# A two-layer decoder step on one core: page table loaded early, GpSimd's layer-1 weight parts in quarters, transfers issued by SyncE

## The chip, the core and the metric

The kernel runs on one core of one Trainium2 chip. The core has five engines, each with an instruction stream of its own, which the document calls as the profile does: PE (TensorE, matrix products), DVE (VectorE), ACT (ScalarE), POOL (GpSimd) and SP (SyncE, which only starts transfers here). Transfers between the chip's memory and the core's own (DMA) are started by an instruction on SP, ACT or POOL and then run by themselves; an engine whose next instruction is the start of a transfer that may not start yet stands still until it may. The metric is the device time of one execution in microseconds (us), and less is better. The numbers are medians of several executions; the profile is of one more execution.

## What is computed

One step of a decoder with two layers, for a prompt of 512 tokens and for 8 sample sequences of 4 new tokens with a past of 1024, all in float32, model width 1024:

```
for layer in range(2):
    h = rms_norm(x, norm_mix[layer])
    z = h @ w_in                                   # one projection for everything in the layer
    t = hgrn2(z) if layer == 0 else sparse_attention(z)   # 6 heads of 128
    c = memory_attention(z)                        # 4 heads of 64 over 256 memory rows
    x = x + concat(t, c) @ w_out[layer]
    h = rms_norm(x, norm_ffn[layer])
    u = h @ w_gate                                 # width 2816
    y = (silu(causal_conv3(u)) * (h @ w_up)) @ w_down
    x = x + y

# sparse_attention, for the samples
ik_past = cache_idx_k[page_table]                  # 8 pages of 128 rows a sequence
score   = sum_h iw[h] * relu(iq[h] . ik)           # then the 256 best rows of a token are chosen
k, v    = cache_k[page_table], cache_v[page_table] # and attention goes over the chosen rows
```

Layer 0's mixer is a gated linear recurrence over chunks of 32 tokens. In layer 1 each token's indexer scores choose the 128 (prompt) or 256 (samples) rows that its attention sees; the keys, values and indexer keys of the past lie in pages, and a table of 64 entries says where. The memory rows of the prompt are projected in each layer, and those of the samples come from a cache. Beside x, the step returns the new keys, values, states and convolution rows.

## The kernel before, in words

The residual x lies feature-major in eight tiles of 128 features by 544 tokens (32 sample tokens, then 512 of the prompt). All weights are one list of 199 units of 128x1024 float32, in the order of their use. `Weights` (716) loads a unit at most three ahead into `raw`, ACT copies it into `whi` in a format of less precision, and the rest, `wlo = raw - whi`, is made by DVE or POOL; `part` (753) says by which. A product over such a unit is three passes on PE (`mm3`): `a<-hi,whi`, `a<-lo,whi` and `a<-hi,wlo`, and these are the bulk of the trace.

The program is written out instruction by instruction, and nothing reorders it afterwards: an engine executes its own in the order in which the Python code reaches them. Two kinds of code call the engines. The main stream goes through the projections. Generators, each a head or a part of one, lie in `Pump` (495) and are moved on between the main stream's products. Which one comes next, and whether DVE or POOL makes a `wlo`, is decided at build time by `Model` (225), a set of clocks moved on by rough costs. `Pump.run`, `finish`, `space` and `drain` are the places at which the main stream lets generators go on.

Weights are loaded by SP, in layer 1 by POOL (`W.queue, W.lead = G, LEAD1`, 1625; back at 2145). Other transfers of the places at hand:

- `sample_kv` (1161) loads keys and values of the cached memory, two transfers for each of eight sequences and each layer, issued by ACT (`S`); `mem_load` (960) the prompt's memory; `ffn` (1180) the convolution's state `cst`. Layer 1's new keys, values and indexer keys (`k_p`, `v_p`, `ik_p` and their `_s`) and two small tables (`tt`, `ex`) also go by ACT.
- The page table is loaded between layer 0's `out_proj` (1172) and the norm before its FFN (1575 to 1593): once as it is into all partitions (`ptb`, 64 entries), and by eight transfers into `ptv`, 16 partitions each. DVE makes row numbers from both, `iidx` for the gathers of indexer keys and `vidx` for those of values. The norm's last part, `Norm._finish` (934), comes behind: column sums on PE, 1/sqrt on DVE (`m__finish`, `rs`), its spread over the partitions on PE (`rb__finish`).
- In layer 1, `sample_scores` (1905) loads 64 key pages by SP (`key_page`, 1600), each by an address that SP reads out of `ptb`, two groups ahead, while attention of the prompt, the selection of rows (`choose_sample`, 1755) and the memory attention run as generators.

In the rows every helper records its instructions at line 398, so the names of the tiles say which step it is.

Of the kernel before, what the change touches and what calls it, by code (L numbers as in the profile page):

```python
# [7 lines left out]
F32 = mybir.dt.float32  # L8
# [25 lines left out]
# ---------------------------------------------------------------- host layout  # L34
# [43 lines left out]
def weight_units(i, order):  # L78
    """the weight blocks in the order in which the program asks for them"""
# [128 lines left out]
TURNS = 2          # selections at work at a time  # L208
# [13 lines left out]
NUNITS = 199  # L222


class Model:
# [89 lines left out]
    def room(self, g, gens):  # L315
        """from when a generator's next step finds the tiles that it takes"""
# [25 lines left out]
    def held_up(self, n, eng):  # L342
        """until when other engines are at work on the part of a tile that is to be written"""
# [58 lines left out]
def place(busy, t, took):  # L402
    """the first time from t on when something is free for so long"""
# [11 lines left out]
def extent(ap):  # L415
    """first and last column and partition of an operand in its tile"""
# [78 lines left out]
class Pump:  # L495
    """Generators of instructions beside the main stream. A generator yields, before each step, the tiles that
    the step reads (None: all that it has given out so far); a step is given out once they are ready."""
    def __init__(self, model):
        self.turn = 0
        self.m, self.gens, self.dv, self.names, self.urgent = model, [], [], {}, []  # L500
# [1712 lines left out]
```

## Time and profile before

| what | value |
|---|---|
| time, median of 3 runs | 1492.95 us (1491.08 to 1493.73) |
| span of the profiled execution | 1500.7 us |
| PE busy | 1434.9 us, 96% |
| DVE, ACT, POOL busy | 803.2, 587.5, 567.3 us |
| layer 0 up to its out_proj | 0 to about 347 us |
| layer 0's FFN | about 353 to 750 us |
| layer 1 up to its out_proj | 750 to about 1050 us |
| layer 1's out_proj and FFN | 1050 to 1500 us |

The profile is of one execution, whose span is 0.5% above the median of the timed runs. Busy times of engines overlap, so they don't add up to the span; what counts is where PE is idle and whom it waits for there. A row of a timeline is a run of like instructions on one engine: when it started, how long it took, the engine, the operation, what it writes `<-` what it reads, how many, and in brackets how long the engine was idle before and what ended that.

### The profile page before, as it was taken

The page shows a single profiled execution, that of the slowest core. Times are in us where ns is not written, and L with a number is a line of the kernel's source. Part 1 is how long each engine was busy: PE and PEld are TensorE (multiplying, and loading weights), DVE is VectorE, ACT ScalarE, POOL GpSimd, SP SyncE. Part 2 cuts the span into 40 slices and gives each one's busy share as a digit, 9 for nine tenths or more (in the row PEclk, how much of TensorE's full clock was granted, in tenths as well). Part 3 has the DMA queues.
Part 4 walks back from the last instruction along what each step waited for, and adds up shares of the span by engine and source line. Part 5 has one row for each costly group of instructions (what it writes and reads, how often), then busy time and mean ns, then how long its engine had stood idle before and what let it go on. Part 6 is the DMA issues. An engine that isn't in the chain of part 4 may idle for free.

```text
span 1500.7 us, 28191 instructions
## 1 busy us (share of the span) xinstructions
PE 1434.9 (96%) x11314; PEld 1345.6 (90%) x11314; DVE 803.2 (54%) x1762; ACT 587.5 (39%) x1064; POOL 567.3 (38%) x600
## 2 busy tenths in 40 slices
PE   8989999998999999999999797689999999999998
PEld 7978889998999999999987775456999999999998
DVE  7466886653444234444469988867444442244431
ACT  5447466332333123333335443466333331133320
POOL 4422444323444124446753444341134440144410
PEclk9999999999999999999999997989999999999999
DMA  5542132321333223224414236631222323232241
GB/s 186 177 156 64 59 117 86 101 85 62 88 95 93 92 73 94 90 85 126 135 54 131 83 115 202 199 127 57 71 76 89 96 85 99 73 95 87 85 121 57
DMA packets 60145, 152.52 MB, mean 102 GB/s; under 512 B 9040, under 2 KB 22960, under 8 KB 60016
## 3 DMA queue, kind: packets, MB, share of 16 engines
q1 hardware_dynamic: 39456, 110.11, 23.9%
q0 software_dynamic: 8208, 26.50, 5.4%
q10 hardware_dynamic: 12352, 14.13, 2.9%
q8 instruction: 89, 1.46, 0.4%
q14 instruction: 40, 0.33, 0.1%
HBM read 142.23 MB, written 8.47 MB: 100 GB/s over the span
## 4 chain that ended last, share of the span: by engine, by line
PE 84%; DVE 11%; issue 2%; ACT 1%; DMA 1%; another core or an unknown queue 0%; ACTq 0%; POOL 0%; SPq 0%; DVEq 0%; POOLq 0%
PE a L398 71%; DVE ple_choose_sample L398 2%; PE u_hgrn_head L398 1%; DVE isc_index_prompt L398 1%; PE id_index_prompt L398 1%; PE mkv L398 1%; PE ao_prompt_attn L398 1%; PE ho_hgrn_head L398 1%; PE ms_prompt L398 1%; PE hgrn_head_samples L398 1%; PE as_prompt_attn L398 1%; DVE t L398 1%; DMA ptv<-pt 1%; DVE lo L398 1%; PE mo_prompt L398 1%
## 5 line engine op out<-in xcount | busy, mean ns | idle before, releaser
L398 PE MATMUL a<-hi,whi 128*128 128x272 f32 x2640 | 556.4, 292 | 1.4 <-DVE t L398 1.0
L398 PE MATMUL a<-lo,whi 128*128 128x272 f32 x2640 | 551.0, 290 | 4.9 <-DVE lo L398 4.6
L398 POOL TENSOR_TENSOR wlo<-raw,whi 128x1024 fp32r<-128x1024 f32 x143 | 342.7, 2397 | 557.3 <-ACT whi L398 551.1
L398 PE MATMUL a<-hi,wlo 128*128 128x272 f32 x2640 | 549.1, 289 | 0.0
L398 PEld LDWEIGHTS a<-hi,whi 128*128 128x128 f32 x2640 | 417.7, 190 | 9.2 <-issue 5.4
L398 PEld LDWEIGHTS a<-lo,whi 128*128 128x128 f32 x2640 | 418.1, 190 | 6.2 <-DVE lo L398 5.6
L398 PEld LDWEIGHTS a<-hi,wlo 128*128 128x128 f32 x2640 | 418.1, 190 | 0.0
L398 ACT ACTIVATE whi<-raw 128x1024 fp32r<-128x1024 f32 (+1 forms) x202 | 209.5, 1038 | 230.9 <-PE a L398 151.3
L398 DVE TENSOR_TENSOR wlo<-raw,whi 128x1024 fp32r<-128x1024 f32 (+1 forms) x59 | 79.7, 1351 | 160.6 <-ACT whi L398 157.7
L398 DVE TENSOR_TENSOR sc<-a,rb 128x544 f32<-128x544 f32 x53 | 38.4, 724 | 116.1 <-PE a L398 114.5
L398 DVE SCALAR_TENSOR_TENSOR conv<-ext,params,conv 128x560 f32<-128x560 f32 x88 | 70.6, 802 | 45.1 <-ACT conv L398 43.6
L398 DVE TENSOR_TENSOR ext<-a,rb 128x240 f32<-128x240 f32 x132 | 37.5, 339 | 105.9 <-PE a L398 102.2
L398 ACT ACTIVATE conv<-ext,params 128x560 f32<-128x560 f32 x44 | 37.6, 855 | 136.2 <-DVE ext L398 132.6
L398 ACT ACTIVATE hi<-sc 128x544 fp32r<-128x544 f32 x44 | 29.0, 658 | 137.3 <-DVE sc L398 137.3
L398 DVE TENSOR_TENSOR x<-a,x 128x544 f32<-128x544 f32 x48 | 34.7, 723 | 80.1 <-PE a L398 72.5
L398 POOL TENSOR_TENSOR sqa<-sqa,sq 128x544 f32<-128x544 f32 x24 | 34.8, 1448 | 110.0 <-ACT sq L398 108.3
L398 DVE TENSOR_TENSOR sc<-sc,conv 128x512 f32<-128x512 f32 x88 | 62.5, 748 | 4.9 <-DVE sc L398 0.5
L398 ACT ACTIVATE conv<-conv 128x560 f32<-128x560 f32 x44 | 29.6, 672 | 73.8 <-DVE conv L398 73.8
L398 ACT ACTIVATE hi<-x,params 128x544 fp32r<-128x544 f32 x32 | 23.9, 745 | 70.4 <-DVE x L398 68.5
L398 DVE TENSOR_TENSOR lo<-sc,hi 128x544 fp32r<-128x544 f32 x44 | 31.9, 725 | 31.9 <-ACT hi L398 31.9
L398 PE MATMUL a<-whi,hi 128*128 128x256 f32 x160 | 46.8, 293 | 0.0
L398 PE MATMUL a<-whi,lo 128*128 128x256 f32 x160 | 45.1, 282 | 0.0
(406 smaller groups left out, 1931.9 us busy)
## 6 DMA issues: line engine op xcount, KB each, us to landing
raw<-w SPq DMA_DIRECT2D x177, 512.0 KB, 3.6
raw<-w POOLq DMA_DIRECT2D x21, 512.0 KB
k_sample_scores<-ckT SPq DMA_DIRECT2D x46, 128.0 KB, 3.5
ck_mem_samples<-cmkT ACTq DMA_DIRECT2D x16, 256.0 KB, 6.2
cv_mem_samples<-cmv ACTq DMA_DIRECT2D x16, 256.0 KB, 4.7
st_s<-hgrn_head_samples POOLq DMA_DIRECT2D x12, 256.0 KB
hgrn_head_samples<-hst SPq DMA_DIRECT2D x10, 256.0 KB, 3.5
ck_sample_scores<-ckT SPq DMA_DIRECT2D x18, 128.0 KB, 2.1
```

The costliest lines, as they stand in the source:

```text
L398: return f(*args, **kw)
```

## The change

Five edits, of which the fourth only removes text (comments).

1. In layer 1, a `wlo` that POOL makes is four instructions of 128x256 instead of one of 128x1024 (`W.piece`). There are 21 of them. Those of DVE, and POOL's in the rest of the program, stay whole.
2. The order of generators is a string (`SCRIPT`), read by `Pump.play`, and `Pump.pick` reads from it which engine takes a `wlo` and two other small steps. Read out engine by engine, PE's order is row for row that of before, and DVE's but for the rows below.
3. The page table comes from the host as one 128x72 array, in which the 64 entries stand in each partition and `ptv`'s eight behind them. One transfer on SP, before layer 0's fifth head, loads it; `page_rows` makes `iidx` and `vidx` ahead of layer 0's `out_proj`.
4. Comments go.
5. All of ACT's transfers but the parameters and rope tables at the start are issued by SP (`Q`), at the same places of the program.

```diff
+    def begin(self, script):
+        self.made = [*self.gens, *self.dv]
+        self.script = iter([c for n, c in re.findall(r"(\d*)(\D)", script) for _ in range(int(n or 1))])
+
+    def play(self):
+        for c in self.script:
+            if c == ".":
+                return
+            g = self.made[LETTERS.index(c)]
+            self.step(g, self.gens if g in self.gens else self.dv)
+
+    def pick(self, c):
+        return c if self.script is None else next(self.script) == "+"
...
     def run(self, *need):
+        if self.script is not None:
+            return self.play()
...
-                (V if model.t["dve"] <= late else G).tensor_sub(lo[:, c:c + n], raw[:, c:c + n], hi[:, c:c + n].bitcast(F32))
+                if pump.pick(model.t["dve"] <= late):
+                    V.tensor_sub(lo[:, c:c + n], raw[:, c:c + n], hi[:, c:c + n].bitcast(F32))
+                    return
+                step = min(n, self.piece)
+                for i in range(c, c + n, step):
+                    G.tensor_sub(lo[:, i:i + step], raw[:, i:i + step], hi[:, i:i + step].bitcast(F32))
...
     def sample_kv(l, b):
         k, v = slot(name="ck"), slot(name="cv")
-        S.dma_start(k[:, :512], a["cmkT"][l, b])
-        S.dma_start(v3(v[:, :512], 2, 256), a["cmv"][l, b].rearrange("(m p) c -> p m c", p=128))
+        Q.dma_start(k[:, :512], a["cmkT"][l, b])
+        Q.dma_start(v3(v[:, :512], 2, 256), a["cmv"][l, b].rearrange("(m p) c -> p m c", p=128))
...
+    def page_rows():
+        p4 = v3(ptb[:, 0:64], 32, 2)
+        for e in range(2):
+            pr = slice(64 * e, 64 * e + 64)
+            V.tensor_scalar(iidx[pr], p4[pr, :, e], 64.0, cc("iota64")[pr], op0=ALU.mult, op1=ALU.add)
+        V.tensor_scalar(vidx[:, 0, :], ptb[:, 64:72], 64.0, cc("iota16"), op0=ALU.mult, op1=ALU.add)
+        for i in range(1, 4):
+            V.tensor_scalar(vidx[:, i, :], vidx[:, 0, :], float(i), None, op0=ALU.add)
...
+        if hd == 4:
+            Q.dma_start(ptb, a["pt"])
...
+    page_rows()
     norm = Norm(gffn[:, 0, :])
     out_proj(0, cat, [*([g] for g in gates), [mg[0], mg[1], mg[4]], mg[2:5]], norm)
     n1 = Norm(gmix[:, 1, :])
-    S.dma_start(ptb, bass.AP(tensor=pt_ap.tensor, offset=pt_ap.offset, ap=[[0, 128], [1, 64]]))
...
-    for s in range(8):
-        S.dma_start(ptv[16 * s:16 * s + 16, :], bass.AP(tensor=pt_ap.tensor, offset=pt_ap.offset + s, ap=[[0, 16], [8, 8]]))
...
-    W.queue, W.lead = G, LEAD1
+    W.queue, W.lead, W.piece = G, LEAD1, 256
...
-            S.dma_start(a["k_p"][256 * i:256 * i + 256].rearrange("(j p) c -> p j c", p=128), v3(kr[i][:, :512], 2, 256))
-        S.dma_start(a["k_s"], kr[2][0:NS, :256])
+            Q.dma_start(a["k_p"][256 * i:256 * i + 256].rearrange("(j p) c -> p j c", p=128), v3(kr[i][:, :512], 2, 256))
+        Q.dma_start(a["k_s"], kr[2][0:NS, :256])
...
-        pt=cont(i["page_table"].reshape(1, 64)),
+        pt=cont(np.concatenate([np.tile(i["page_table"].reshape(1, 64), (128, 1)),
+                                np.repeat(i["page_table"].reshape(8, 8).T, 16, axis=0)], 1)),
```

DVE's order before, at the end of layer 0's out_proj (`x` is the residual, `sqa` the sum of its squares, `m__finish` the norm's rows):

```order
L398 TENSOR_TENSOR x_89<-a_3986,x_89 128x544
L398 SCALAR_TENSOR_TENSOR lo_4037<-x_89,params_79,hi_4036 128x544
L398 TENSOR_TENSOR sqa_3520<-sqa_3520,sq_4038 128x544
L398 TENSOR_SCALAR iidx<-ptb,consts_81 64x32 x2
L398 TENSOR_SCALAR vidx<-ptv,consts_81 128x8
L398 TENSOR_SCALAR vidx<-vidx 128x8 x3
L398 TENSOR_SCALAR m__finish_1_4120<-st__finish_1_4111 128x5
```

And now, at the end of layer 0's heads, where the six rows stand between the gates (`lo_gate`, `sc`) and ahead of the first `x` of out_proj; behind `sqa`, `m__finish` follows at once:

```order
L420 TENSOR_TENSOR sc_3429<-sc_3429,on_hgrn_head_1_3052 128x544
L420 TENSOR_SCALAR iidx<-ptb,consts_81 64x32 x2
L420 TENSOR_SCALAR vidx<-ptb,consts_81 128x8
L420 TENSOR_SCALAR vidx<-vidx 128x8 x3
L420 TENSOR_TENSOR lo_gate_1_3556<-sc_3429,hi_gate_1_3555 128x544
L420 TENSOR_TENSOR sc_3521<-sc_3521,on_hgrn_head_1_3539 128x544
L420 TENSOR_TENSOR lo_gate_1_3592<-sc_3521,hi_gate_1_3591 128x544
L420 TENSOR_TENSOR x_82<-a_3531,x_82 128x544
```

So the six rows moved from ahead of the norm to ahead of out_proj. POOL's order now, in layer 1's projections, where it loads weights (`raw`), makes low parts and the second half of a rotation (`rq`):

```order
L420 TENSOR_TENSOR wlo_9021<-raw_9018,whi_9020 128x256 x4
L420 DMA raw_9114<-w 128x1024
L420 DMA raw_9116<-w 128x1024
L420 DMA raw_9118<-w 128x1024
L420 TENSOR_TENSOR wlo_9133<-raw_9114,whi_9132 128x256 x4
L420 DMA raw_9139<-w 128x1024
L420 TENSOR_TENSOR rq_9268<-rq_9268,t_5_9269 128x544
L420 TENSOR_TENSOR wlo_9275<-raw_9116,whi_9274 128x256 x4
```

Each low part was one row of 128x1024 at the same place. ACT's order before, in layer 1 where the keys are done (`kr`), with the transfers between its own instructions:

```order
L398 ACTIVATE sr_9815<-ss_sample_scores_4_10650 128x256
L398 DMA k_p<-kr_10030 128x2x256
L398 DMA k_p<-kr_10031 128x2x256
L398 DMA k_s<-kr_10032 32x256
L398 ACTIVATE kT_10033<-kT_keys_1_10684 128x512
L398 ACTIVATE kT_10066<-kT_keys_2_10690 128x512
L398 ACTIVATE ktn<-kTn_keys_1_10696 128x64
L398 DMA ck_mem_samples_1_10755<-cmkT 128x512
L398 DMA cv_mem_samples_1_10756<-cmv 128x2x256
```

They moved to SP, whose order there is now (`ck_sample_scores` is a tile of two key pages, and TENSOR_LOAD reads a page's address from the table):

```order
L420 DMA ck_sample_scores_21_10708<-ckT 128x256
L420 DMA k_p<-kr_10066 128x2x256
L420 DMA k_p<-kr_10067 128x2x256
L420 DMA k_s<-kr_10068 32x256
L1659 TENSOR_LOAD ptb
L1659 ISA x2
L420 ISA
L420 DMA ck_sample_scores_22_10748<-ckT 128x256
```

What moved here is that the pages behind now come after the three stores; the first batch of eight `ck` and `cv` of the memory follows four pages later, the second twelve pages after that, and six pages come last.

## Rows read from the trace of the kernel before

**Rows 1.** the page's first part: busy us (share) xinstructions of each engine

```profile
PE 1434.9 (96%) x11314; PEld 1345.6 (90%) x11314; DVE 803.2 (54%) x1762; ACT 587.5 (39%) x1064; POOL 567.3 (38%) x600
```

**Rows 2.** windows: stretch, us, busy of PE PEld DVE ACT POOL, clock, DMA

```profile
340.00:360.00 20.00, 14.95 (x107) 14.24 (x107) 6.36 (x25) 4.89 (x8) 5.29 (x6) 0.83 0.19 63
...
750.00:870.00 120.00, 106.97 (x770) 93.89 (x770) 101.96 (x239) 55.97 (x137) 55.38 (x67) 0.96 0.27 84
870.00:1050.00 180.00, 149.22 (x1073) 104.49 (x1073) 140.23 (x464) 94.88 (x261) 68.75 (x76) 0.89 0.45 146
```

**Rows 3.** chain of waits, 340 to 360 us: start us, us, what

```profile
339.67 9.91 DMA ptv<-pt
```

**Rows 4.** timeline of PE, 345 to 372 us: start us, us, instructions [idle before <- releaser]

```profile
347.10 0.41 PE L398 MATMUL a<-hi,wlo 128*128 128x272 f32 x2
352.57 1.36 PE L398 MATMUL rb__finish<-consts,rs 128*128 128x128 f32 x5 [5.05 <-DVE rs L398]
...
357.58 0.41 PE L398 MATMUL a<-hi,wlo 128*128 128x272 f32 x2
```

**Rows 5.** the same around the second FFN, 1100 to 1112 us

```profile
1105.72 0.41 PE L398 MATMUL a<-hi,wlo 128*128 128x272 f32 x2
...
1108.77 0.41 PE L398 MATMUL a<-hi,wlo 128*128 128x272 f32 x2
```

**Rows 6.** timeline of DVE, 330 to 358 us

```profile
349.65 0.23 DVE L398 TENSOR_SCALAR vidx<-ptv,consts 128x8 int32<-128x8 int32 x1 [10.00 <-DMA ptv<-pt]
```

**Rows 7.** groups of POOL's instructions, 750 to 1050 us: count, busy us, mean ns, idle before

```profile
L398 POOL TENSOR_TENSOR wlo<-raw,whi 128x1024 fp32r<-128x1024 f32 x21 | 50.0, 2383 | 37.6 <-ACT whi L398 37.6
...
L398 POOL TENSOR_TENSOR kr<-v,tt 128x128 f32<-128x128 f32 x8 | 4.5, 601 | 2.8 <-DVE v L398 2.8
```

**Rows 8.** timeline of DVE, 835 to 842 us

```profile
837.70 2.26 DVE L398 TENSOR_TENSOR ple_choose_sample<-consts,ple_choose_sample 128x7 int32<-128x7 int32 x1
```

**Rows 9.** timeline of POOL, 835 to 842 us

```profile
837.54 2.39 POOL L398 TENSOR_TENSOR wlo<-raw,whi 128x1024 fp32r<-128x1024 f32 x1
```

**Rows 10.** timeline of DVE, 888 to 892 us

```profile
890.57 0.16 DVE L398 TENSOR_TENSOR ple_choose_sample<-consts,ple_choose_sample 128x3 int32<-128x3 int32 x1
```

**Rows 11.** timeline of DVE, 757 to 764 us

```profile
759.59 3.43 DVE L398 TENSOR_SCALAR m_index_keys<-m_index_keys 128x5 f32<-128x5 f32 x4
```

**Rows 12.** timeline of DVE, 950 to 968 us

```profile
962.86 3.18 DVE L398 TENSOR_SCALAR p_prompt_attn<-p_prompt_attn,m_prompt_attn 128x256 f32<-128x256 f32 x1
```

**Rows 13.** timeline of DVE, 905.5 to 911 us

```profile
908.88 0.45 DVE L398 TENSOR_TENSOR ple_choose_sample<-ple_choose_sample 128x1 int32<-128x1 int32 x1
```

**Rows 14.** timeline of DVE, 765 to 774 us

```profile
767.94 4.67 DVE L398 TENSOR_TENSOR t_index_keys<-ikt_index_keys,tt 128x32 f32<-128x32 f32 x10
```

**Rows 15.** timeline of POOL, 765 to 774 us

```profile
769.32 2.44 POOL L398 TENSOR_TENSOR wlo<-raw,whi 128x1024 fp32r<-128x1024 f32 x1
```

**Rows 16.** timeline of ACT, 918 to 958 us

```profile
930.26 0.63 ACT L398 ACTIVATE hi<-mem 128x512 fp32r<-128x512 f32 x1 [5.36 <-DMA cv_mem_samples<-cmv]
...
951.94 0.60 ACT L398 ACTIVATE p_prompt_attn<-p_prompt_attn,m_prompt_attn,rqs 128x256 f32<-128x256 f32 x1 [4.82 <-DMA cv_mem_samples<-cmv]
```

**Rows 17.** timeline of PE, 945 to 970 us

```profile
953.59 0.49 PE L398 MATMUL ao_prompt_attn<-pt_prompt_attn,v 128*128 128x128 f32 x2 [2.08 <-ACT pt_prompt_attn L398]
...
964.11 1.25 PE L398 MATMUL ss_sample_scores<-k_sample_scores,qS 128*32 128x256 f32 x15 [0.93 <-ACT ct_prompt_attn L398]
```

**Rows 18.** timeline of SP's transfer issues, 926 to 966 us

```profile
926.87 29.86 SPq L398 DMA_DIRECT2D k_sample_scores<-ckT  x19
```

**Rows 19.** the page's sixth part: issues, KB each, median us from issue to landing

```profile
k_sample_scores<-ckT SPq DMA_DIRECT2D x46, 128.0 KB, 3.5
```

**Rows 20.** timeline of ACT, 36 to 75 us

```profile
68.81 1.06 ACT L398 ACTIVATE whi<-raw 128x1024 fp32r<-128x1024 f32 x1 [4.22 <-DMA cv_mem_samples<-cmv]
```

**Rows 21.** windows in layer 0, columns as in rows 2

```profile
60.00:80.00 20.00, 20.00 (x193) 17.56 (x193) 11.64 (x29) 6.56 (x18) 5.97 (x9) 1.00 0.78 273
```

**Rows 22.** windows around the end of layer 0's heads, columns as in rows 2

```profile
288.00:294.00 6.00, 6.00 (x50) 6.00 (x49) 3.46 (x3) 3.22 (x6) 2.86 (x3) 1.00 0.28 87
```

More of the change, by code (lines that the diff above doesn't have):

```diff
@@ L1 @@
+import re
 import numpy as np
@@ L499, in __init__ @@
         self.turn = 0
+        self.script, self.made = None, []
         self.m, self.gens, self.dv, self.names, self.urgent = model, [], [], {}, []
@@ L504, in make @@
         self.names[name] = n = self.names.get(name, 0) + 1
-        return Gen(it, after, f"{name}{n}", pri, margin)
+        g = Gen(it, after, f"{name}{n}", pri, margin)
+        self.made.append(g)
+        return g
+    def begin(self, script):
[9 more added lines that the diff above has]
+        return c if self.script is None else next(self.script) == "+"
     def add(self, it, after=None, pri=5, margin=0):
@@ L600, in finish @@
     def finish(self, g):
+        if self.script is not None:
+            return self.play()
         while not g.done:
@@ L610, in space @@
     def space(self, tag):
+        if self.script is not None:
+            return self.play()
         m = self.m
@@ L620, in drain @@
     def drain(self):
+        if self.script is not None:
+            return self.play()
         while self.gens:
@@ L640, in program @@
     pump = Pump(model)
+    if plan is not None:
+        pump.begin(SCRIPT)
     uid = {}
@@ L719, in __init__ @@
             self.raw, self.parts, self.kept = {}, {}, {}
-            self.queue, self.lead = Q, LEAD0
+            self.queue, self.lead, self.piece = Q, LEAD0, 1024
             self.whole = list(plan.whole) if plan else []
@@ L861, in scale_rows @@
     def scale_rows(p, r):
-        if model.t["act"] < model.t["dve"]:
+        if pump.pick(model.t["act"] < model.t["dve"]):
             S.activation(p, p, AF.Copy, scale=r)
@@ L951, in scaled @@
         t = slot(name="sc")
-        if model.t["dve"] > max(model.t["pe"], model.t["act"]) + BUSY:
+        if pump.pick(model.t["dve"] > max(model.t["pe"], model.t["act"]) + BUSY):
             S.activation(halves(t), ac, AF.Copy)
@@ L961, in mem_load @@
         t = slot(name="mem")
-        S.dma_start(v3(t[:, :512], 2, 256), a["memT"][:, 2 * len(raw):2 * len(raw) + 2, :])
+        Q.dma_start(v3(t[:, :512], 2, 256), a["memT"][:, 2 * len(raw):2 * len(raw) + 2, :])
         raw.append(t)
@@ L1182, in ffn @@
         cst = slot(name="cst")
-        S.dma_start(cst[:, :NF * 16], a["cst"][l])
+        Q.dma_start(cst[:, :NF * 16], a["cst"][l])
         SE = 514
@@ L1542, in gate @@
         cat[hd] = yield from split_in(sg)
+    ptb = cp.tile([128, 72], I32, name="ptb")
+    iidx = cp.tile([128, 32], I32, name="iidx")
+    vidx = cp.tile([128, 4, 8], I32, name="vidx")
+    def page_rows():
[6 more added lines that the diff above has]
+            V.tensor_scalar(vidx[:, i, :], vidx[:, 0, :], float(i), None, op0=ALU.add)
     memraw = []
@@ L1577, in program @@
     n1 = Norm(gmix[:, 1, :])
-    ptb = cp.tile([128, 64], I32, name="ptb")
-    pt_ap = a["pt"]
-    S.dma_start(ptb, bass.AP(tensor=pt_ap.tensor, offset=pt_ap.offset, ap=[[0, 128], [1, 64]]))
-    iidx = cp.tile([128, 32], I32, name="iidx")
-    p4 = v3(ptb, 32, 2)
-    for e in range(2):
-        pr = slice(64 * e, 64 * e + 64)
-        V.tensor_scalar(iidx[pr], p4[pr, :, e], 64.0, cc("iota64")[pr], op0=ALU.mult, op1=ALU.add)
-    ptv = cp.tile([128, 8], I32, name="ptv")
-    for s in range(8):
-        S.dma_start(ptv[16 * s:16 * s + 16, :], bass.AP(tensor=pt_ap.tensor, offset=pt_ap.offset + s, ap=[[0, 16], [8, 8]]))
-    vidx = cp.tile([128, 4, 8], I32, name="vidx")
-    V.tensor_scalar(vidx[:, 0, :], ptv, 64.0, cc("iota16"), op0=ALU.mult, op1=ALU.add)
-    for i in range(1, 4):
-        V.tensor_scalar(vidx[:, i, :], vidx[:, 0, :], float(i), None, op0=ALU.add)
     def gather(out, src, idx):
@@ L1621, in program @@
     for i, t in enumerate(tt):
-        S.dma_start(t, a["ttab"][:, i, :])
+        Q.dma_start(t, a["ttab"][:, i, :])
     qtab = [tt[j // 4][:, 128 * (j % 4):128 * (j % 4) + 128] for j in range(5)]
     itab = [tt[1][:, 128 + 64 * j:192 + 64 * j] for j in range(5)]
-    W.queue, W.lead = G, LEAD1
+    W.queue, W.lead, W.piece = G, LEAD1, 256
     cat = [None] * 8
@@ L1651, in index_keys @@
         yield from key_rope([ikv], pc("g_ik"), itab, rs, 1, 64, [ikr])
-        S.dma_start(a["ik_p"].rearrange("(j p) c -> p j c", p=128), v3(ikr[:, :256], 4, 64))
-        S.dma_start(a["ik_s"], ikr[0:NS, 256:320])
+        Q.dma_start(a["ik_p"].rearrange("(j p) c -> p j c", p=128), v3(ikr[:, :256], 4, 64))
+        Q.dma_start(a["ik_s"], ikr[0:NS, 256:320])
         b, b2 = bank("ikT"), bank("ikT")
@@ L2114, in program @@
                 ex = slot(name="ex")
-                S.dma_start(ex[0:NS, :256], a["expand"])
+                Q.dma_start(ex[0:NS, :256], a["expand"])
                 V.tensor_copy(eb, ex[0:NS, :256])
@@ L2132, in values @@
                 for i in range(2):
-                    S.dma_start(a["v_p"][256 * i:256 * i + 256].rearrange("(j p) c -> p j c", p=128), v3(row[i][:, :512], 2, 256))
-                S.dma_start(a["v_s"], row[2][0:NS, :256])
+                    Q.dma_start(a["v_p"][256 * i:256 * i + 256].rearrange("(j p) c -> p j c", p=128), v3(row[i][:, :512], 2, 256))
+                Q.dma_start(a["v_s"], row[2][0:NS, :256])
             token_major(proj_tm("dtm", 1024, xs=h), values, 0)
@@ L2144, in program @@
             mem_load(memraw)
-    W.queue, W.lead = Q, LEAD0
+    W.queue, W.lead, W.piece = Q, LEAD0, 1024
     model.keep, model.main = 0, MAIN0
```

21 lines of the change are left out of this document (added).

## The prediction

> **What bounds the kernel now.** The page's first part comes first: TensorE (PE) is busy 1434.9 us of a span of 1500.7 [rows 1], so at most 66 us are to be had unless PE itself runs quicker. The stages say where they lie [rows 2]: PE is busy 14.95 of 20 us at 340 to 360, 106.97 of 120 at 750 to 870 and 149.22 of 180 at 870 to 1050. These lack 5.05, 13.03 and 30.78 us, and their granted clock is 0.83, 0.96 and 0.89, between the two levels of 1.2 and 2.4 GHz: part of PE's busy time there is spent at the lower one. In the two late stretches VectorE (DVE) is nearly as full as PE, 101.96 of 120 and 140.23 of 180, so what DVE waits for counts there.
>
> The first place is a single stall. The chain of waits has the transfer ptv<-pt for 9.91 us from 339.67 [rows 3]; behind it DVE's first vidx instruction has waited 10.00 us and starts at 349.65 [rows 6]; and PE, in the first norm before an FFN, ends its last pair of products of out_proj and waits 5.05 us for DVE's rs [rows 4]. The rest is spread, and I read it by timelines of single engines.
>
> **Page table (term A, -7.4).** The six page instructions stand in DVE's order ahead of the norm's m__finish, so one small late transfer holds the norm. The same norm before the second FFN has none. From the start of the last pair of the output projection to that of the ninth pair behind rb__finish it is 357.58 - 347.10 = 10.48 us in the first [rows 4] and 1108.77 - 1105.72 = 3.05 in the second [rows 5]: the same PE rows, one time with the wait and the low clock that follows it. The difference is 7.43 us. With the wait gone, next late is what the second norm shows, and that leaves no gap. I take -7.4, with 1 us either way.
>
> The table now comes by one transfer on SyncE (SP) at head 4, before the fifth of six heads, and is read behind the sixth. Its six DVE instructions stand between the gates of layer 0; where the heads end PE is busy 6.00 of 6 and DVE 3.46 [rows 22], so I cost them at 0. If a gate behind them were late, they would cost what they take: six times at most the 0.23 of the first vidx [rows 6], some 1.4.
>
> **Quarters (term B, -7).** A DVE instruction that begins as a long GpSimd (POOL) instruction begins ends only with it: 128x7 int32 at 837.70 took 2.26 us [rows 8] while POOL's wlo ran from 837.54 for 2.39 [rows 9], and the same instruction with 128x3 took 0.16 [rows 10]. Of layer 1's 21 wlo on POOL [rows 7] I count 16 that hold a DVE instruction so, by 1.9 to 2.8 us, some 34 us in all; the first held one is in the four of 759.59 that took 3.43 together [rows 11], the last the one of 3.18 at 962.86 [rows 12]. What does a short POOL instruction do? While eight kr of 128x128 run, 601 ns each [rows 7], a DVE instruction of one column took 0.45 [rows 13], so it was held by at most 0.45, not 2.1.
>
> A quarter's time, from two rows of the same operation [rows 7]: (2383 - 601)/(1024 - 128) = 1.99 ns a column, so 601 + 128 x 1.99 = 856 ns, four 3.42 us, 1.04 more than the whole, 22 us on POOL in all. POOL is busy 55.38 of 120 and 68.75 of 180 [rows 2], so this is hidden as long as a weight's low part is not what PE waits for.
>
> What DVE saves depends on what follows the held one. Where it is followed by instructions that POOL does not hold (8 of 16, selection and softmax work as in rows 8), one hold of 2.1 becomes one of about 0.6: 1.5 saved. In two mixed places I take 0.8. In the other six DVE runs through instructions with two inputs, as the ten t_index_keys that took 4.67 [rows 14] across the wlo of 2.44 at 769.32 [rows 15]; there each quarter can hold the next one, and I take 0. DVE saves 8 x 1.5 + 2 x 0.8 = 13.6. Only part is on PE's path: in these 300 us PE lacks 43.8 while DVE lacks 57.8 [rows 2], so neither rules all the time. I take half, -7. The ends are -13.6, and +3, if six dense places lose 0.5 each to more changes of hand.
>
> The Trainium skill (SBUF — State Buffer, Terms) says that the port pair of VectorE and GpSimd is locked exclusively, for a full instruction, and that the loser blocks completely. Rows 8 and 9 agree, 2.26 us against 2.39. By the rule alone four quarters are four locks, and the term would be 0 wherever DVE's work wants those ports throughout.
>
> **ScalarE freed (term C, -2).** ScalarE (ACT) issued eight memory-key and memory-value transfers in a row at two places of layer 1 and stood behind them 5.36 us before 930.26 and 4.82 before 951.94 [rows 16]. Only behind the second does PE wait, 2.08 us before 953.59, for ACT's pt_prompt_attn [rows 17]. That is -2.1; the ends are 0 (something else is late there) and 5.36 + 4.82 = -10.2. In layer 0 ACT stood 4.22 behind such a batch at 68.81 [rows 20], but PE is busy 20.00 of 20 there [rows 21]: 0.
>
> The Trainium skill (DMA: Bandwidth & Descriptors, Issuing engines are not separate DMA queues) says that starting transfers on several engines saves only the time of starting them, usually small beside the transfer. By that the whole term would be near 0; rows 16 show 4.82 us of an engine that was not small.
>
> **SP loaded (term D, +2).** SP now issues these, and they are queued among the key pages of the sample scores. Behind k_p come 19 pages in 29.86 us [rows 18]; two batches of eight and three stores join them. An issue takes at most the even share of ACT's second wait, 4.82/8 = 0.6 us, so 19 x 0.6 = 11.4 us more [rows 16]. The last page is issued by 926.87 + 29.86 = 956.73 and lands 3.5 us later [rows 18, 19]; the group of scores that needs it begins at 964.11 [rows 17], so 964.11 - 956.73 - 3.5 = 3.9 us are spare. If pages are issued without a pause, the queue ends 11.4 later and PE waits 11.4 - 3.9 = 7.5; if SP's present pauses take them up, 0. A page takes 29.86/19 = 1.57 us on average, with its address read into a register, against 0.6 for a plain issue, so pauses for free page tiles are in it, how long the rows don't say. The ends are 0 and +7.5; nearer to the first, since the spare time and the pauses add up, I take +2.
>
> In layer 0 SP's weight loads now stand behind the same batches. The cover is PE's full 20.00 of 20 [rows 21]; if it were gone, it would cost up to the 4.22 us of the batch [rows 20].
>
> **Sum.** -7.4 - 7 - 2 + 2 = -14.4. The profiled execution's 1500.7 us become 1486.3. The median of before, 1492.95, is 0.5% below that execution; the same microseconds from it give **1478.5**.
>
> **Rivals.** *Quarters give nothing.* Each quarter holds a DVE instruction again, as rows 14 and 15 would have it for work with two inputs. For it speaks that POOL's total rises; against it the 0.45 of rows 13. Then A and C and D stay: -7.4 - 2 + 2, **1485.5**.
>
> *DVE was the bound after all.* All 13.6 of B reach PE, C gives 5, and part of the clock comes back: 0.89 granted over 180 us [rows 2] means PE's work would need less time at the full level; an estimate of a quarter of the 19.8 us lost (180 x 0.11) is 5. Then -7.4 - 13.6 - 5 + 2 - 5 = -29 with everything, some -25 with overlap, **1468**. For it speaks DVE's load, against it that PE stands idle for several other releasers.
>
> *SP becomes the bound (slower).* A page behind a moved transfer waits for that transfer's turn. If each batch and the stores stop SP as long as ACT was stopped by a batch, 5.36 [rows 16], and the page slots then come late as well, so that the last page falls behind by three such stops and the 11.4 us of issuing, 27.5 in all, less the 3.9 spare: PE waits 23.6, and in the sum +23.6 - 7.4 - 7 - 2 = +7: **1500**. It decides against the change once the last page comes over 3.9 + 16.4 = 20.3 us late. Against it: SP has pauses, and the transfers are the same bytes.
>
> *The stall is replaced.* The norm's wait goes but another takes its place, as a late weight behind SP's batch in layer 0 (4.22) and pages late by 7.5, with B down to -3: -7.4 + 4.2 + 7.5 - 2 - 3 = -0.7: **1492**. That the change doesn't do what it says I rule out for its order: the page rows, the quarters and the transfers do stand elsewhere on their engines.
>
> **How the numbers follow.** Forecast 0.47; quarters nothing 0.19; DVE the bound 0.16; stall replaced 0.09; SP the bound 0.09. Under 0.2%, 3 us, a measurement of this kernel can't be told from no change. So faster 0.82, same 0.09, slower 0.09. The range reaches to 1465 and to 1489: below, the larger gain but for its far end; above, 1485.5 with the 3 us that B may cost. It leaves out the last two rivals and a little below.
>
> **What would show it.** Right, A: no idle of PE before the first rb__finish, and DVE's vidx at about 290 us without a wait; 3.1 us in place of 10.48. B: no DVE instruction of a few columns above 1 us beside a wlo, and DVE's busy sum from 750 to 1050 (242.2 now) down by some 13 us; wrong, if the sum stays. C: ACT without the 4.82. D: the last page issued by about 960 of the old times, and the last group of scores released by something else. Wrong altogether, if PE's idle time in the two late stretches stays at 44 us though each engine's own waits are gone, or if SP's page groups are what PE waits for.

## The result, and the profile after

The changed kernel takes 1481.34 us (median of 6 runs, 1477.83 to 1486.18) where before takes 1493.34 beside it: a ratio of 0.9919, with a 95% interval of 0.9902 to 0.9936, or -12.1 us (-9.5 to -14.6). The forecast was 1478.5, -14.4.

The profiled execution has a span of 1479.6 us, 21.1 less than the profiled one of before. That is more than the times say, and the section on the stall below tells why. PE's row of the page, which answers to [rows 1]:

```profile
PE 1428.4 (97%) x11314; PEld 1341.1 (91%) x11314; DVE 797.0 (54%) x1762; ACT 587.3 (40%) x1064; POOL 578.5 (39%) x663
```

PE executes the same 11,314 instructions in the same order, so the start of the n-th can be compared between two traces. This gives what each stage of the program gained or lost against the trace of before, in us (stages by the times of before; the column 815-870 is a part of the one before it; e1 to e12 are the runs below):

| kernel | 1-345 | 345-358 | 358-745 | 745-870 | 815-870 | 870-955 | 955-1012 | 1012-1490 |
|---|---|---|---|---|---|---|---|---|
| after | +4.3 | -6.6 | -0.5 | -6.7 | -6.3 | -0.6 | -10.3 | -0.6 |
| e5, after again | +4.6 | -6.6 | +0.1 | -6.1 | -5.6 | -1.0 | +0.5 | +0.6 |
| e1, page table late | +3.1 | +0.1 | +0.4 | -6.5 | -6.3 | -2.0 | +1.7 | +1.6 |
| e2, whole parts | +5.6 | -6.6 | +0.3 | +0.7 | +0.1 | +1.5 | +5.5 | +1.6 |
| e3, ACT issues | +1.4 | -6.6 | +0.1 | -3.9 | -5.7 | -3.0 | +3.3 | +1.0 |
| e4, order alone | +1.5 | +0.2 | +0.2 | +2.6 | +0.9 | -0.4 | +3.9 | +0.2 |
| e6, quarters alone | +5.8 | +0.3 | 0.0 | -3.4 | -5.7 | -3.0 | +0.5 | +1.2 |
| e7, SyncE alone | +4.0 | +0.3 | -0.1 | +0.1 | +0.1 | -0.4 | +0.2 | +1.5 |
| e8, layer 0's memory by ACT | +3.1 | -6.6 | 0.0 | -6.4 | -6.3 | -2.9 | +0.7 | +1.8 |
| e9, halves | -0.2 | -6.6 | -0.5 | -3.1 | -2.8 | -0.2 | -10.0 | -0.6 |
| e10, eighths | +1.8 | -6.6 | -0.5 | -8.8 | -8.5 | -2.2 | -10.3 | -0.6 |
| e11, plain rows | +2.9 | -6.6 | -0.5 | -6.5 | -6.3 | -1.4 | -11.9 | -0.6 |
| e12, eighths, ACT issues | +0.8 | -6.6 | +0.2 | -6.4 | -8.1 | -2.6 | +1.0 | +0.2 |

e4 runs before's own instructions, so a difference of 2 to 4 us in its row is chance. Two columns stand clear of that: 345 to 358, where every kernel with the early page table gains 6.62 us and no other gains at all, and 815 to 870, where the steps of the samples' selection lie. There all seven kernels with quarters gain 5.6 to 6.3, halves 2.8, eighths 8.1 and 8.5, and the four with whole parts lie between 0 (before) and +0.9.

The wider column 745 to 870 looks less even, because e3, e4, e6 and e12, in which ACT issues the transfers, lose 2.0 to 2.6 us of it between 745 and 784, ahead of those steps. Before, in which ACT issues them too, doesn't lose this, and no kernel whose layer-1 transfers SP issues loses more than 0.6 there. Whether the issuing or the chip is the reason stays open.

**The norm.** The timeline of PE in the changed kernel, around layer 0's norm, against [rows 4]:

```profile
351.35 0.41 PE L420 MATMUL a<-hi,wlo 128*128 128x272 f32 x2
351.60 0.77 PE L420 MATMUL rb__finish<-consts,rs 128*128 128x128 f32 x5
...
353.87 0.49 PE L420 MATMUL a<-hi,whi 128*128 128x272 f32 x2 [0.54 <-DVE ext L420]
...
355.19 0.41 PE L420 MATMUL a<-hi,wlo 128*128 128x272 f32 x2
```

rb__finish follows without a wait, and from the last pair to the ninth it is 355.19 - 351.35 = 3.84 us in place of 10.48. The chain of waits there (start, us, what) has no transfer any more:

```profile
344.78 6.98 PE a L420 x54
351.76 0.45 PE rb__finish L420 x4
...
352.24 0.61 ACT rb L420
...
352.87 0.86 DVE ext L420 x3
```

What is late next is ACT's copy of rb and DVE's ext behind it, 0.54 us of PE. The six page rows now lie here on DVE, and PE beside them (first two rows: timeline of DVE; third: a window, us, busy of PE, PEld, DVE, ACT, POOL, clock):

```profile
291.17 3.71 DVE L420 TENSOR_SCALAR iidx<-ptb,consts 64x32 int32<-64x32 int32 x2
294.89 0.23 DVE L420 TENSOR_SCALAR vidx<-ptb,consts 128x8 int32<-128x8 int32 x1
```

```profile
290.00:300.00 10.00, 10.00 (x83) 10.00 (x82) 7.40 (x11) 5.03 (x8) 5.24 (x3) 1.00 0.18 53
```

The two iidx took 3.71 us (1.36 and 2.34), and PE is busy 10.00 of 10 all the same. POOL's timeline says why they were so slow: one ends with POOL's `sc`, the other with a low part, which in layer 0 is whole. It is the hold of term B.

```profile
291.13 1.36 POOL L420 TENSOR_TENSOR sc<-sc,rb 128x544 f32<-128x544 f32 x1 [4.92 <-ACT sc L420]
292.46 2.38 POOL L420 TENSOR_TENSOR wlo<-raw,whi 128x1024 fp32r<-128x1024 f32 x1
```

**The quarters.** The instruction of [rows 8], at the same place, and POOL's low part beside it [rows 9]; two timelines:

```profile
831.11 1.03 DVE L420 TENSOR_TENSOR ple_choose_sample<-ple_choose_sample 128x7 int32<-128x7 int32 x2
832.17 0.59 DVE L420 TENSOR_TENSOR ple_choose_sample<-consts,ple_choose_sample 128x7 int32<-128x7 int32 x1
832.68 0.54 DVE L420 TENSOR_SCALAR_CACHE_REDUCE ple_choose_sample<-row_index_sample,ple_choose_sample,ple_choose_sample 128x264 f32<-128x264 f32 x1
```

```profile
830.72 1.33 POOL L420 TENSOR_TENSOR rq<-rq,t 128x544 f32<-128x544 f32 x1 [2.04 <-DVE t L420]
832.02 2.80 POOL L420 TENSOR_TENSOR wlo<-raw,whi 128x256 fp32r<-128x256 f32 x4
```

0.59 in place of 2.26, while POOL works 2.80 us in place of 2.39; the instruction behind, with 0.54, is not held by the next quarter. The same holds in every trace: of the 17 instructions of this kind (128x7 int32), the five that meet a low part take 2.21 to 2.27 us in the four kernels with whole parts and 0.59 to 0.61 in the seven with quarters. Ahead of each of the five another one still takes 0.96 us or more and ends with POOL's rotation `rq`, as in the first rows here; the change does not touch `rq`. In the two calls of PE at this step it waited 1.00 us before, at the second, and waits 0.23 now, at the first (timelines of PE, before first):

```profile
841.67 0.39 PE L398 MATMUL ple_choose_sample<-ple_choose_sample,consts 128*128 128x3 f32 x2 [1.00 <-DVE ple_choose_sample L398]
```

```profile
834.75 0.61 PE L420 MATMUL ple_choose_sample<-ple_choose_sample,consts 128*128 128x4 f32 x4 [0.23 <-ACT ple_choose_sample L420]
```

Where DVE runs through instructions with two inputs, nothing changed. The ten t_index_keys of [rows 14] took 4.67 and now take 4.63, beside four quarters of 2.99 together (DVE, then POOL):

```profile
764.90 4.63 DVE L420 TENSOR_TENSOR t_index_keys<-ikt_index_keys,tt 128x32 f32<-128x32 f32 x10
```

```profile
766.28 2.99 POOL L420 TENSOR_TENSOR wlo<-raw,whi 128x256 fp32r<-128x256 f32 x4
```

The stretches of the changed kernel that hold the program's part of [rows 2] from 750 to 1050 (columns as there):

```profile
747.00:860.50 113.50, 104.97 (x771) 92.30 (x771) 92.59 (x239) 56.22 (x137) 61.32 (x103) 0.97 0.28 89
860.50:960.00 99.50, 78.89 (x610) 59.75 (x613) 84.45 (x300) 45.28 (x120) 45.15 (x72) 0.86 0.58 183
960.00:1028.40 68.40, 64.48 (x467) 41.51 (x460) 54.10 (x165) 49.51 (x142) 27.15 (x29) 0.98 0.36 117
```

DVE is busy 92.59 + 84.45 + 54.10 = 231.1 us in them, 11.1 less than the 242.2 of before, and 9.4 of that is in the first: 92.59 for 101.96. There PE lacks 113.50 - 104.97 = 8.5 us where it lacked 13.0; its busy time is 2.0 us less as well, at a granted clock of 0.97 for 0.96. So of the 6.5 us by which this stretch is shorter, 4.5 are waits of PE and 2.0 its own work.

**The transfers.** ACT no longer stands behind transfers. The first row is ACT's, the second PE's, in the changed kernel, where [rows 16, 17] have 4.82 and 2.08 us; the third is PE's next wait as it was before:

```profile
939.70 0.60 ACT L420 ACTIVATE p_prompt_attn<-p_prompt_attn,m_prompt_attn,rqs 128x256 f32<-128x256 f32 x1 [2.64 <-DVE m_prompt_attn L420]
```

```profile
945.31 0.47 PE L420 MATMUL apt_prompt_attn<-consts,p_prompt_attn 128*128 128x128 f32 x2 [3.47 <-DVE p_prompt_attn L420]
```

```profile
955.44 0.69 PE L398 MATMUL apt_prompt_attn<-consts,p_prompt_attn 128*128 128x128 f32 x2 [1.36 <-DVE p_prompt_attn L398]
```

PE's wait of 2.08 is gone, and two instructions further it waits 3.47 in place of 1.36, so 2.11 us come back at once: DVE scales p_prompt_attn only behind its selection of rows, which ACT's freedom does not move. In all 14 traces the two waits add up to 3.43 to 3.47 us, whoever issues; e3, where ACT issues again, has them divided as before (timeline of PE):

```profile
941.80 0.49 PE L420 MATMUL ao_prompt_attn<-pt_prompt_attn,v 128*128 128x128 f32 x2 [2.23 <-ACT pt_prompt_attn L420]
943.49 0.69 PE L420 MATMUL apt_prompt_attn<-consts,p_prompt_attn 128*128 128x128 f32 x2 [1.21 <-DVE p_prompt_attn L420]
```

SP's timeline in the changed kernel, against [rows 18], and the last group of scores:

```profile
924.28 12.92 SPq L420 DMA_DIRECT2D k_sample_scores<-ckT  x12
...
943.47 6.85 SPq L420 DMA_DIRECT2D k_sample_scores<-ckT  x6
```

```profile
953.76 1.25 PE L420 MATMUL ss_sample_scores<-k_sample_scores,qS 128*32 128x256 f32 x15 [1.94 <-ACT ct_prompt_attn L420]
```

Twelve pages behind each other take 12.92 us, 1.08 each, where the nineteen of before took 1.57: the pauses were there. The last is issued by 943.47 + 6.85 = 950.3, 3.4 us ahead of the group, and a page lands 2.1 us after its issue here (median). The group waits 1.94 us for ACT; in e4, whose instructions are those of before, it waits 1.95, so SP's load is not the reason.

### The profile page after: what moved, and what is told of

It reads as the page before. It is cut to its first block, busy times and chain, and to the rows that moved or that the text cites. A ratio compares the mean times of both kernels' runs of the same rounds, so it can differ in the third digit from the quotient of the medians.

```text
span 1479.6 us, 28277 instructions
## 1 busy us (share of the span) xinstructions
PE 1428.4 (97%) x11314; PEld 1341.1 (91%) x11314; DVE 797.0 (54%) x1762; ACT 587.3 (40%) x1064; POOL 578.5 (39%) x663
## 4 chain that ended last, share of the span: by engine, by line
PE 84%; DVE 7%; issue 3%; POOL 2%; ACT 2%; DMA 1%; SPq 0%; ACTq 0%; POOLq 0%; DVEq 0%
PE a L420 73%; PE u_hgrn_head L420 1%; POOL wlo L420 1%; PE id_index_prompt L420 1%; PE ho_hgrn_head L420 1%; PE ms_prompt L420 1%; PE hgrn_head_samples L420 1%; PE as_prompt_attn L420 1%; DVE lo L420 1%; PE mkv L420 1%; PE mo_prompt L420 1%; PE sc_hgrn_head L420 1%; DMA raw<-w 1%; PE ao_prompt_attn L420 1%; PE mpt_prompt L420 1%
## 5 line engine op out<-in xcount | busy, mean ns | idle before, releaser
L420 POOL TENSOR_TENSOR wlo<-raw,whi 128x1024 fp32r<-128x1024 f32 (+1 forms) x206 | 353.9, 1729 | 560.1 <-ACT whi L420 536.0
L420 DVE TENSOR_TENSOR sc<-sc,conv 128x512 f32<-128x512 f32 x88 | 65.8, 786 | 4.6
```

The lines of the kernel that those rows point to most:

```text
L420: return f(*args, **kw)
```

## The experiments

The experiments ran on four chips. The kernel before took 1493 us beside the result and on the chip of e9 to e11 (1492.5), and 1510 to 1513 on the chips of the other runs, which are slower by about 1% throughout. So each run is compared with the before beside it, by the ratio, and its microseconds are that ratio's.

**e1: the page table late again.** Of the changed kernel, the early load and page_rows are taken back:

```diff
-        if hd == 4:
-            Q.dma_start(ptb, a["pt"])
...
-    page_rows()
...
+    S.dma_start(ptb, bass.AP(tensor=pt_ap.tensor, offset=pt_ap.offset, ap=[[0, 128], [1, 64]]))
+    for s in range(8):
+        S.dma_start(ptv[16 * s:16 * s + 16, :], bass.AP(tensor=pt_ap.tensor, offset=pt_ap.offset + s, ap=[[0, 16], [8, 8]]))
```

> The changed kernel with the page table loaded as before (nine transfers on ScalarE between out_proj and the norm, page rows ahead of the norm); quarters and SyncE's issuing stay. Theory (each part is worth its own sum; the page stall is worth 7 of the 12 us): -5 us against before, about 1488, with 5 us of TensorE idle again before the first rb__finish. Rival (the stall is replaced by another wait as soon as it goes, so the page table is worth little): -10 us or more, about 1483.

Measured: 0.9916 (0.9901 to 0.9932), -12.7 us. The expected number was missed, and taken alone -12.7 is the rival's; but both were set against the -12.1 of the result, and where before takes 1510 us too, the changed kernel itself gives -16.2 (e5). By these times the page table is worth 3.5 us, with an uncertainty as large; by the trace it is 6.62 + 0.10 = 6.7 at its place, while the other columns of e1 and e5 differ by 1.5 us at most, within chance. PE's timeline has the wait back:

```profile
355.87 1.36 PE L420 MATMUL rb__finish<-consts,rs 128*128 128x128 f32 x5 [5.25 <-DVE rs L420]
```

**e2: whole low parts.**

```diff
-    W.queue, W.lead, W.piece = G, LEAD1, 256
+    W.queue, W.lead, W.piece = G, LEAD1, 1024
```

> The changed kernel with GpSimd's layer-1 low parts whole (128x1024); early page table and SyncE's issuing stay. Theory (quarters are worth 5 to 7 us, at the places in the samples' selection where TensorE waits for one held VectorE instruction): -5 to -7 against before, about 1487, and TensorE's gaps of 1.0 us at the selection's steps are back. Rival (quarters move holds about and give nothing; the rest of layer 1's gain is ScalarE no longer standing behind transfers): -11 or more, about 1482.

Measured: 0.9966 (0.9949 to 0.9983), -5.1 us, as the theory has it; against e5 the quarters are worth 11 us by the times, and by the column 745 to 870 it is 0.7 + 6.1 = 6.8 (815 to 870: 0.1 + 5.6 = 5.7). The gaps are back:

```profile
841.64 0.39 PE L420 MATMUL ple_choose_sample<-ple_choose_sample,consts 128*128 128x3 f32 x2 [0.99 <-DVE ple_choose_sample L420]
```

**e3: ACT issues its transfers again.** At the twelve lines of the change, but for the page table:

```diff
-        Q.dma_start(k[:, :512], a["cmkT"][l, b])
+        S.dma_start(k[:, :512], a["cmkT"][l, b])
...
-        Q.dma_start(a["k_s"], kr[2][0:NS, :256])
+        S.dma_start(a["k_s"], kr[2][0:NS, :256])
```

> The changed kernel with ScalarE issuing all the transfers that it issued before; early page table (on SyncE) and quarters stay. Theory (ScalarE freed and SyncE loaded cancel, as terms C and D): -12 within 2 us, about 1481. Rival A (ScalarE's freedom gave 5 us or more): -7 or less, about 1486. Rival B (SyncE's load costs, the moved transfers delay weights in layer 0): better than the changed kernel by 3 us or more, about 1478.

Measured: 0.9883 (0.9869 to 0.9898), -17.7 us. Against the result that looks like rival B; against e5, beside which it belongs, it is equal within the intervals.

**e4: the order alone.** The edits of e1, e2 and e3 together; a single execution.

> The written-down order alone, all three other parts undone: every engine's order is row for row that of before. A second profile of the same instructions, to see which differences between two profiles are chance. Theory (the 2.9 us that layer 0 lost at 80 to 103 us and the 4 us stall of all engines at 972 us, present in before alone, are chance): within 0.3% of before, and at least one of the two does not show. Rival (they belong to the order of transfers): both as in the profile of before.

Measured: 1510.6 us in a single run where before takes 1513.3. The 972 us stall shows, with 3.26 us of PE; of the 2.3 us that after lost between 80 and 100 us, 1.4 are lost here too, with before's own instructions. So that loss is chance, by more than half at least; the stall did not go away. The theory held for the first and not for the second.

**e5: the changed kernel again.** No edit.

> The changed kernel itself, for its place among the others on one chip, and for a second profile. Theory (the parts add up: page table -6.6, quarters -10, SyncE's issuing +2): -14 against before, and the profile has the two stalls of all engines (about 4.9 and 3.1 us, between 955 and 1010 us) that its first profile lacked, so its layer 1 gains less than the 18.8 us seen there. Rival (the three parts together do away with the stalls): -18 or more, and no such stall in this profile either.

Measured: 0.9893 (0.9875 to 0.9910), -16.2 us. Both stalls show in its profile, and from 745 to 1012 it gains 6.1 + 1.0 - 0.5 = 6.6 us where the first profile showed 17.6. The theory held in the profile; the time lies between the two expectations.

**e6: quarters alone.** The edits of e1 and e3 together.

> Before with nothing but the quarters (and the written-down order, which changes no row). Theory: -8 to -11, most of it between 800 and 870 us, where the selection of the samples runs. Rival (quarters give nothing by themselves): within 2 us of before.

Measured: 0.9958 (0.9939 to 0.9976), -6.3 us: not nothing, and a little under the theory. The trace puts 6.4 us of it between 745 and 955, and 5.7 of these between 815 and 870.

**e7: SyncE's issuing alone.** The edits of e1 and e2 together.

> Before with nothing but SyncE issuing ScalarE's transfers. Theory (terms C and D cancel): within 2 us of before. Rival A (ScalarE's freedom is worth 4 us or more): -4 or less. Rival B (SyncE's issuing costs, by lower clock in layer 0 where the first batch of memory transfers now starts at 30 instead of 38 us): +2 to +5, with 2 to 4 us lost before 340 us.

Measured: 1.0010 (0.9998 to 1.0023), +1.5 us. It gains nothing, as the theory says; rival A is out. The 4.0 us that its profile lost before 345 us are no proof of rival B, since e6, with ACT issuing, lost 5.8: in that column the kernels in which ACT issues all of its transfers lie between 0 (before) and +5.8, those in which SP does between -0.2 and +5.6. A cost of 1 or 2 us there is not excluded.

**What the times give, pair by pair.** Runs that differ in one part alone put the page table at 3.5 (e5 and e1), 6.6 (e2 and e7) and 11.4 us (e3 and e6); the quarters at 11.1 (e5 and e2), 14.2 (e1 and e7) and 6.3 (e6 and before); SyncE's issuing at +1.5 (e7 and before), +1.5 (e5 and e3) and -6.4 (e1 and e6). Each has an uncertainty of 2 to 4 us, and most pairs span two chips, which may add to it. The last value contradicts the two before it by more than that, and why stays open; the value farthest from its neighbours shares e6 in each of the three parts. So the sizes in this document rest on the traces' columns, and the times confirm them roughly. No run has the early page table alone.

**e8: layer 0's memory transfers by ACT.**

```diff
-        Q.dma_start(k[:, :512], a["cmkT"][l, b])
+        (Q if l else S).dma_start(k[:, :512], a["cmkT"][l, b])
```

> The changed kernel with ScalarE issuing the memory's keys and values of layer 0 only; all else as changed. Theory (the 3 us that the profiles with SyncE's issuing lose before 340 us belong to those sixteen transfers): 2 to 4 us better than the changed kernel, with TensorE's clock at 1.00 at 24 to 36 us. Rival (the low clock there is chance): equal to the changed kernel within 2 us.

Measured: 0.9907 (0.9888 to 0.9926), -14.0 us, not better than e5's -16.2: the rival. Windows of 24 to 36 us in e8, after, e6 and e10 (columns as in [rows 2]):

```profile
24.00:36.00 12.00, 12.00 (x93) 11.76 (x93) 9.44 (x37) 4.27 (x9) 4.08 (x12) 0.86 0.36 113
```

```profile
24.00:36.00 12.00, 11.53 (x90) 10.80 (x89) 9.31 (x39) 4.28 (x9) 3.51 (x8) 0.86 0.84 281
```

```profile
24.00:36.00 12.00, 12.00 (x81) 11.57 (x81) 9.36 (x38) 3.89 (x8) 3.81 (x10) 0.72 0.32 110
```

```profile
24.00:36.00 12.00, 10.72 (x94) 10.25 (x93) 9.40 (x38) 4.28 (x9) 3.92 (x11) 1.00 0.88 287
```

The granted clock there was 0.86, 0.86, 0.72 and 1.00. With SP's early batch (DMA 0.84, 0.88) it was once low and once full; without it (e8 and e6, DMA 0.36 and 0.32) it was no higher than in after, where the theory wanted 1.00. Before and e4, whose instructions are the same, have 0.86 and 1.00. So the clock's dips do not follow the transfers.

**e9: halves, and e10: eighths.** The first of these lines in e9, the second in e10:

```diff
-    W.queue, W.lead, W.piece = G, LEAD1, 256
+    W.queue, W.lead, W.piece = G, LEAD1, 512
+    W.queue, W.lead, W.piece = G, LEAD1, 128
```

> The changed kernel with two pieces of 128x512 instead of four of 128x256. Theory (a held VectorE instruction waits for one piece and then goes on, so the hold shrinks with the piece): a hold of about 1.1 instead of 0.6, so 2 to 3 us behind the changed kernel, and the selection's steps at 825 to 865 us lose 0.5 us each. Rival (any cut will do, since what counts is that GpSimd lets go once): equal to the changed kernel within 1 us.

> The changed kernel with eight pieces of 128x128. Theory (hold shrinks with the piece, but each piece costs GpSimd its start): holds of 0.3, another 1 us gained at the selection's steps and 1 to 2 lost where TensorE waits for GpSimd's low part, whose time grows to 3.5 us or more; within 2 us of the changed kernel. Rival (shorter is better throughout): 3 us better or more.

Measured: halves 0.9931 (0.9915 to 0.9947), -10.3 us; eighths 0.9884 (0.9862 to 0.9906), -17.3; quarters, beside a like before, -12.1. The order is that of the pieces, though neighbours' intervals overlap, so that by the times alone quarters can be told neither from halves nor from eighths. As they stand, halves are 1.8 us behind quarters, just short of e9's theory, and eighths 5.2 ahead, which is the rival's number in e10. The same held instruction in e9 and in e10:

```profile
829.42 1.14 DVE L420 TENSOR_TENSOR ple_choose_sample<-consts,ple_choose_sample 128x7 int32<-128x7 int32 x1
```

```profile
827.70 0.32 DVE L420 TENSOR_TENSOR ple_choose_sample<-consts,ple_choose_sample 128x7 int32<-128x7 int32 x1
```

And POOL's pieces in layer 1 of after, e9 and e10 (groups: count, busy us, mean ns):

```profile
L420 POOL TENSOR_TENSOR wlo<-raw,whi 128x256 fp32r<-128x256 f32 x80 | 57.3, 742 | 35.6 <-ACT whi L420 35.6
```

```profile
L420 POOL TENSOR_TENSOR wlo<-raw,whi 128x512 fp32r<-128x512 f32 x40 | 51.2, 1297 | 36.8 <-ACT whi L420 36.8
```

```profile
L420 POOL TENSOR_TENSOR wlo<-raw,whi 128x128 fp32r<-128x128 f32 x166 | 72.3, 467 | 29.1 <-ACT whi L420 29.1
```

Pieces of 2383, 1297, 742 and 467 ns held the instruction for 2.26, 1.14, 0.59 and 0.32 us in all: it goes on when the piece ends that it ran into. Halves, quarters and eighths gain 3.1, 6.7 and 8.8 us at 745 to 870, and 2.8, 6.3 and 8.5 of these at 815 to 870. That eight pieces take 72.3/166 x 8 = 3.5 us of POOL did not turn it round: the loss that e10's theory set against the gain does not show.

**e11: plain rows in place of gathers.**

```diff
-                gather(t[:, :512], a["cv"], vidx[:, n, 4 * g + b4:4 * g + b4 + 1])
+                k = 128 * (4 * (4 * g + b4) + n)
+                G.dma_start(t[:, :512], a["cv"][k:k + 128, :])
```

> The changed kernel with the 32 gathers of cached values by row numbers replaced by plain transfers of 128 rows in a row, issued by GpSimd at the same places and of the same bytes, so the samples' attention uses other rows than the table and the values part of the page table goes unused. Theory (the stall of TensorE, VectorE and ScalarE of 4 to 5 us behind the memory attention comes with the gathers' making on GpSimd): no idle time over 3 us of all three between 950 and 1000 us, and 4 to 8 us better than the changed kernel. Rival (it comes with the bytes, or with neither): the stall stays, and the time is equal within 2 us but for the shorter instructions on GpSimd.

Measured: 0.9911 (0.9892 to 0.9931), -13.3 us, equal to the changed kernel. No stall shows, but neither does it in e9 and e10, which ran beside it with all their gathers. This run decides nothing.

**e12: eighths, and ACT issues.** The edits of e3 and e10 together.

> The changed kernel with eight pieces of 128x128 and with ScalarE issuing the transfers that it issued before: early page table and shorter pieces alone. Theory (SyncE's issuing is worth nothing to within 2 us, and eighths are 2 to 5 us better than quarters): -17 to -20 against before. Rival (eighths gained by SyncE's issuing, which leaves ScalarE free where VectorE is now quicker): -12 to -14.

Measured: 0.9894 (0.9871 to 0.9917), -16.0 us, between the two expectations and equal to e5. So e3, e5, e10 and e12 can't be told from each other by the ratio. Of those that ran where before takes 1493 us, eighths are the fastest, 1475.23 us; that they beat quarters rests on the column 815 to 870, where both kernels with eighths (8.1 and 8.5) lie clear of all seven with quarters (5.6 to 6.3).

**The stall that made the profiles differ.** Between 955 and 1012 us, after gained 10.3 us on before in the traces. Of this, 4.05 and 2.35 us of PE are two stalls that before's trace has and after's has not; the remaining 3.9 us are not assigned. e5 runs the same instructions as after and has them, here on PE and DVE, with POOL's gathers beside it:

```profile
966.86 0.66 PE L420 MATMUL apt_prompt_attn<-consts,p_prompt_attn 128*128 128x128 f32 x2 [4.04 <-issue]
```

```profile
966.23 0.48 DVE L420 TENSOR_SCALAR mo_mem_samples<-mob_mem_samples,m_mem_samples 128x256 f32<-128x256 f32 x1 [3.91 <-remote]
```

```profile
963.34 0.94 POOL L420 DMA_INDIRECT cv_sample_values<-cv,vidx  x1 [0.30 <-issue]
964.59 0.94 POOL L420 DMA_INDIRECT cv_sample_values<-cv,vidx  x1 [0.30 <-issue]
```

PE, DVE and ACT stand for some 4 us, released by nothing that the trace names, while POOL goes on. It shows in all nine profiles taken where before takes 1510 us, and in one of five where it takes 1493, which is that of before. So the change does not remove it where before takes 1510 us. Where before takes 1493, the one profile of before has it and the four of kernels with the change lack it, and the traces alone can't clear the change there; but before's profiled span, 1500.7 us, is longer than its timed runs beside the result (1491.1 to 1500.3), and the times give 12.1 us where the two profiles give 21.1. That speaks for chance. What it waits for stays open.

## Why the prediction was right

The time fell in the range, on the side and near the size that was forecast; the terms did so unequally.

- **Page table (A): right, 0.8 us too large.** 6.62 for 7.43. The second FFN's norm, from which the remainder of 3.05 was taken, doesn't show ext's wait of 0.54, and the remainder was 3.84. e1 brings the wait back.
- **Page rows: the cover was right, the price was not.** Two iidx alone took 3.71 us, over the end of 1.4 for all six. The price was taken from a vidx beside which POOL did nothing long; here the two ran into POOL's `sc` and a whole low part, the very hold of term B. PE's full 10.00 of 10 hid it.
- **Quarters (B): right in place and size.** -7 was forecast, and the stage 745 to 870 gained 6.1 to 6.7 in after and e5 (3.4 and 3.9 in e6 and e3, for the loss ahead of the selection's steps; 5.6 to 6.3 in all from 815 on). That the size fits is in part luck: the half of DVE's 13.6 that was to reach PE was a choice between two ends, not worked out. The split was right as well: sparse places gained, as in 832.17, and dense ones did not, as in 764.90. DVE saved 11.1 us for 13.6. A quarter took 742 ns where the two rows of POOL gave 856. One of the 16 counted holds was counted wrongly: the one of [rows 12] stands beside a wlo of out_proj, behind the place where `W.piece` is 1024 again, and is still there (timeline of DVE in after):

```profile
952.52 3.17 DVE L420 TENSOR_SCALAR p_prompt_attn<-p_prompt_attn,m_prompt_attn 128x256 f32<-128x256 f32 x1
```

- **ScalarE freed (C): the step that failed.** The 2.08 us went as forecast, and 2.11 came back at PE's next wait. The step took the wait as PE's loss without asking what PE needs next: DVE's p_prompt_attn, whose start did not depend on ACT. It was 0, the end that the prediction had named and not taken. e3 and e7 agree, and in every trace the two waits add up to the same 3.4 to 3.5.
- **SyncE loaded (D): 0 for +2.** SP's 19 pages had more pause in them than was allowed for: 1.08 us each when they follow closely.
- **The sum.** -6.6 - 6.4 + 0 + 0 = -13, against -12.1 (-9.5 to -14.6) in the result and -16.2 (-13.6 to -18.9) in e5. C and D were each 2 us off, to opposite sides; that this left the sum as it was is luck.
- **The rivals.** "Quarters give nothing" is out by e2 and e6. "SP becomes the bound" is out by SP's rows and e7. "DVE was the bound after all" holds in part: e10 shows that still shorter holds give PE 2 us more in the same stage. The stall was not replaced, but for 0.54 us.

## What to carry to other kernels

Ask of each wait removed what the waiting engine needs next, and when that is ready: the page table's wait had nothing behind it and gave what it cost, ACT's had a wait of DVE right behind it and gave nothing. Where two engines hold each other up, shorter instructions on the one cost it little (here 2.80 us for 2.39) and free the other, but only where the other does not run into the next piece at once. Two profiles of the same instructions can differ by several microseconds; compare stage by stage along one engine's unchanged order, and trust a column only if a second profile shows it.

## What was not expected of the hardware

A held VectorE instruction is released at the end of the GpSimd piece that it met, down to pieces of 467 ns, where it took 0.32 us in all, and in the selection GpSimd's next piece did not hold the instruction behind it. The granted clock of TensorE between 24 and 36 us was 0.72, 0.86 or 1.00 in runs whose TensorE instructions there were the same, and it did not follow who started a batch of transfers. And there is the stall of three engines of 3 to 6 us, with its cause open.
